# Half of the spare raw buffer for the second output weights' blocks, one sample's rows loaded behind them, and the last pages joined, in the last stage of a hybrid decoder step

## The chip, the cores and the metric

The kernel runs on one core of a Trainium2 chip. The metric is the device time of one execution in microseconds (us). The core has five engines with instruction queues of their own: PE (TensorE, matmuls and transposes; PEld is its weight load), DVE (VectorE), ACT (ScalarE), POOL (GpSimd) and SP (SyncE, which here only issues transfers). An engine works through its queue in order, and semaphores tie the queues together. DMA transfers are issued by SP and by POOL.

## The reference, cut to what matters

One step of a decoder layer for a prompt of 1,024 rows and for eight samples of one row each. All of them are projected, mixed by three head groups, and sent through one output projection:

```python
cat = concat([o_nsa * silu(z_nsa), o_rw * silu(z_rw), o_mem * silu(z_mem)])   # width 1024
return cat @ w_out                                                            # (1024, 1024), plus the residual
```

The change lies where two pieces of this meet, the prompt's output projection and the NSA group of the eight samples. For one sample (`nsa_decode_seq`), `pool[pt_row]` gathers eight pages of 128 past rows by the page table; each row holds k and v for compression and k and v for selection:

```python
cmp2 = compress(rows)                     # 32-row blocks, stride 16, through a small MLP -> compressed k, v
p    = softmax(q . ck)                    # over the compressed blocks
imp  = p @ ov                             # importance of the 16 blocks of 64 rows
sel  = top-16 blocks (first, last two forced)
o    = g0 * (p @ cv) + g1 * (softmax(q . k_sel) @ v_sel) + g2 * window
```

Everything is in float32. The large matmuls are done in three parts: each operand is split into a high part and a low part, and high x high, high x low and low x high are summed.

## The kernel before, in words

The kernel has three stages. The change touches only the last (`phase3`), which runs from about 817 us of the profiled execution to its end.

Two pieces of work share the engines there. **The fill** is the prompt's output projection (`out_prompt`): 16 tiles, eight row blocks for the second half of the output columns (weights W1) and then eight for the first half (weights W0). A tile is 24 matmuls called `p_out` (eight blocks k of the contraction, three parts each). Around it stand a split of the next `cat` block on ACT (`chi`) and DVE (`clo`), a load of the residual (`xres`) and a store, both issued by POOL. **The main line** is the samples' NSA group (`sample_nsa`). It takes the samples in two rounds, 0 to 3 (a=0) and 4 to 7 (a=1). Per sample `squeeze` runs the compression's first layer as 32 matmuls `p_hid`, 16 in the program's text; per round `p_ss` gives the scores of the selected rows, and `nsa_four` goes on with `p_co`, `p_ckT`, `p_cs`, `p_cT`, `p_imp` (twice), `p_PT`, `p_os`, `p_oT`, each a short piece of PE with a DVE and ACT piece behind it. The DVE piece behind the second `p_imp` is the longest: the scores `s_sel`, their maximum `rs_m`, ACT's exponential, and the scaling of `s_sel`, which `p_PT` needs.

The order on PE is written out by hand. The main line is a generator that yields numbers of microseconds; after each yield as many groups of three `p_out` are placed as fill that many by a clock of the program's own. So the yields (`WAIT` after each `squeeze`, and the constants in `nsa_four`) say how much fill covers the work of the other engines. The instructions of the other queues are ordered by a scheduler at build time, main line first.

Three things about memory matter.

- **Weights.** `wo_half` loads a block k of W1 or W0 as 128 x 512 raw numbers, then splits it: ACT makes `woh`, DVE makes `wol`. W1's eight raw blocks go to `raw`, a buffer of two halves (`raw[:, 0]` and `raw[:, 1]`, called `wraw` in the profile). W0's raw blocks go, by POOL's queue, to `wor`, a pool of three buffers. The split parts of W0 take the place of W1's, block by block: block k of W0 can be split when the last tile with W1 has used block k. Four blocks of W1 are loaded a second time for the samples' own projection (`again`, `wob`, raw parts in `big[:, 0]`), and four more by the `wor` pool.
- **Pages.** A sample's pages go to two tiles of 128 x 2048, X (for the compression) and KV (for the selection), each made up of eight pages. `big` has five such tiles (`pg` in the profile), to which come two from the attention stage's buffers and the two halves of `raw`. `load(s)` brings X and KV of a page in one DMA of 256 KB (line 1856); `load_x` and `load_kv` bring one of them, 128 KB each (line 1860).
- **SP's order.** SP issues pages and weights in program order, each page behind a read of the page table.

Of the kernel before, what the change touches and what calls it, by code (L numbers as in the profile page):

```python
# [10 lines left out]
F32 = mybir.dt.float32  # L11
# [25 lines left out]
RATE = {i: (0.8, 0.8, 1, 1) if i > 3 else (1.5, 1.5, 1.5, 0) for i in range(8)}  # L37
WAIT = (15.0, 5.0, 5.0, 0.0, 0.0, 0.0, 9.0, 2.0)
WARM = 34
# [75 lines left out]
class Step:  # L115
# [1759 lines left out]
    def sample_nsa(self):  # L1875
# [3 lines left out]
        with ExitStack() as ctx:  # L1879
# [4 lines left out]
            self.W1 = self.wo_half(self.wo_tiles(self.wop), 1, nc.sync, range(8),  # L1884
                                   lambda k: raw[:, k // 4, k % 4 * 512:k % 4 * 512 + 512])
            vn = dp.tile([128, 2, 128], F32, name="v_new")
            new = O["nsa_rows_sample"]
# [5 lines left out]
            for a in range(2):  # L1893
                for k in range(4):
                    s = 4 * a + k
# [3 lines left out]
            with P("snsx") as xp:  # L1899
                big = xp.tile([128, 5, 2048], F32, name="pg")  # L1900

                at = {1: (0, 2), 2: (1, 3), 3: (0, 4)}
                kvs = lambda x: x.rearrange("p (n c) -> p n c", n=8)
# [21 lines left out]
                for a in range(2):  # L1925
                    hid = dp.tile([128, 4, 2, 64], F32, name="shid")
                    if a == 0:
                        for s in range(4):
                            if s:
                                load(s)  # L1930
                            squeeze(s, hid)
                            yield WAIT[s]
                        for s in (4, 5):
                            self.pages(s, big[:, 5 - s], raw[:, s - 4])
                            X[s], KV[s] = big[:, 5 - s], kvs(raw[:, s - 4])
                        load_x(7, self.arena(0, "pg")[:])
                    else:
                        squeeze(4, hid)
                        load_x(6, big[:, 1])
                        load_kv(6, big[:, 2])  # L1940
                        load_kv(7, big[:, 3])
                        for s in (5, 7, 6):
                            squeeze(s, hid)
                            yield WAIT[s]
                        again = [self.k1p.tile([128, 2048], F32R, name="wob", tag=f"k{j}") for j in (0, 2)]
                        parts = iter([x[:, k * 512:k * 512 + 512] for x in again for k in range(4)])
                        W1 = self.wo_half(lambda name: next(parts), 1, nc.sync, range(4, 8),
                                          lambda k: big[:, 0, k * 512:k * 512 + 512])
                    VS = [KV[s] for s in range(4 * a, 4 * a + 4)]
                    pS = [self.pS.tile([128, 512], F32, name="p_ss", tag="s") for _ in range(2)]  # L1950
                    for h in range(2):
                        for k in range(4):
                            PE.matmul(pS[h][32 * k:32 * k + 32], self.qb[:, 4 * a + k, :], VS[k][:, 4 * h:4 * h + 4, 0:128],
                                      start=True, stop=True)
                    yield from self.nsa_four(a, hid, pS, VS, vn, dp)
                    if a == 0:
                        self.sample_cats()
                        yield None
# [4 lines left out]
    def nsa_four(self, a, hid, pS, VS, vn, dp):  # L1963
# [13 lines left out]
        o = self.norm_rope(ck[:].rearrange("p s d -> p (s d)")[:, None, :], 3, 1, 4, 9)  # L1977
        yield 7.0
        pk = self.pT.tile([128, 4, 128], F32, name="p_ckT", tag="t")
# [3 lines left out]
        V.tensor_copy(kt[:], pk[:64])  # L1983
        yield 1.3
        pc = self.pM.tile([128, 128], F32, name="p_cs", tag="m")
# [31 lines left out]
        V.tensor_scalar(sc[:], sc[:], self.gr[:, a, 0:1], None, op0=OP.mult)  # L2017
        yield 7.5
        srcs = [sl[:, j * 128:(j + 1) * 128] for j in range(8)] + [sc[:]]
# [12 lines left out]
        V.scalar_tensor_tensor(oS[:], vn[:, a, :], sl[:, 1024:1025], po[:], op0=OP.mult, op1=OP.add)  # L2032
        yield 1.3
        pt = self.pM.tile([128, 4, 32], F32, name="p_oT", tag="m")
# [163 lines left out]
    def wo_half(self, tiles, n, queue, ks=range(8), raws=None):  # L2198
        nc = self.nc
        out = {}  # L2200
        for k in ks:
            wl, wh = tiles(f"wol{k}"), tiles(f"woh{k}")
            raw = self.wst.tile([128, 512], F32, name="wor")[:] if raws is None else raws(k - ks[0])
            self.last_wor = queue.dma_start(raw, self.I["w_out"][0, k * 128:(k + 1) * 128, n * 512:(n + 1) * 512])
            nc.scalar.activation(wh, raw, AF.Copy, scale=0.5)  # L2205
            nc.vector.scalar_tensor_tensor(wl, raw, 0.5, wh.bitcast(F32), op0=OP.mult, op1=OP.subtract)  # L2206
            out[k] = wh, wl
        return out
# [67 lines left out]
    def out_prompt(self):  # L2276

        yield from self.out_proj_prompt(1, self.W1)
        self.W0 = self.wo_half(self.wo_tiles(self.wop), 0, self.nc.gpsimd)
        self.half = 1  # L2280
        yield from self.out_proj_prompt(0, self.W0)
# [117 lines left out]
```

## Time and profile before

| | |
|---|---|
| median of 3 runs | 976.06 us (974.77 to 979.17) |
| the profiled execution: its own time | 983.03 us |
| its span, from the first to the last instruction | 981.3 us |
| mean TensorE clock granted | 0.984 |
| PE busy | 939.0 us (96%) |
| DVE busy | 656.6 us (67%) |
| ACT busy | 443.1 us (45%) |
| DMA moved | 103.82 MB, mean 106 GB/s |

Times are in us of the profiled execution, counted from the start of its span. In the timeline a row is: start, duration, engine, line, operation, what it writes and reads, count, and in brackets the idle time of the engine before it with what ended that. In the chain of waits a row is start, duration, what. In the windows a row is a stretch, its length, then busy time of the engines (with the number of instructions), the clock granted to PE (1.00 is full), the mean busy share of the 16 DMA engines, and GB/s. Matmul ends are modelled and overlap the next one's start, so the distance from start to start is what one costs.

### The profile page before, as it was taken

The page shows a single profiled execution, that of the slowest core. Times are in us where ns is not written, and L with a number is a line of the kernel's source. Part 1 is how long each engine was busy: PE and PEld are TensorE (multiplying, and loading weights), DVE is VectorE, ACT ScalarE, POOL GpSimd, SP SyncE. Part 2 cuts the span into 40 slices and gives each one's busy share as a digit, 9 for nine tenths or more (in the row PEclk, how much of TensorE's full clock was granted, in tenths as well). Part 3 has the DMA queues.
Part 4 walks back from the last instruction along what each step waited for, and adds up shares of the span by engine and source line. Part 5 has one row for each costly group of instructions (what it writes and reads, how often), then busy time and mean ns, then how long its engine had stood idle before and what let it go on. Part 6 is the DMA issues. An engine that isn't in the chain of part 4 may idle for free.

```text
span 981.3 us, 24739 instructions
## 1 busy us (share of the span) xinstructions
PE 939.0 (96%) x9851; PEld 796.3 (81%) x9851; DVE 656.6 (67%) x2025; ACT 443.1 (45%) x990; POOL 178.9 (18%) x270
## 2 busy tenths in 40 slices
PE   7999999989999998999998999999999999998997
PEld 7998888868898887778887888888888887876775
DVE  6768669846593897644438776765768986356454
ACT  5755224232432342223435766667567675223311
POOL 2000000000000000000103444445446663112010
PEclk8999999999999999999997999999999999999999
DMA  8331303311331126146238325141110139875611
GB/s 288 87 87 33 92 21 114 97 52 55 86 99 36 40 81 156 45 120 184 61 94 234 108 66 178 62 121 40 52 38 16 43 90 272 272 235 173 202 67 36
DMA packets 134092, 103.82 MB, mean 106 GB/s; under 512 B 34833, under 2 KB 121368, under 8 KB 133848
## 3 DMA queue, kind: packets, MB, share of 16 engines
q1 hardware_dynamic: 129016, 90.53, 31.4%
q0 software_dynamic: 3200, 10.49, 3.0%
q8 instruction: 78, 1.28, 0.5%
q10 hardware_dynamic: 1760, 1.21, 0.4%
q14 instruction: 38, 0.31, 0.1%
HBM read 83.61 MB, written 22.78 MB: 108 GB/s over the span
## 4 chain that ended last, share of the span: by engine, by line
PE 72%; DVE 15%; ACT 6%; DMA 3%; issue 2%; SPq 1%; POOL 0%; DVEq 0%; ACTq 0%; POOLq 0%
PE p_pr L87 20%; PE p_pr L284 7%; PE p_out L87 6%; PE p_s L87 6%; PE p_pT L87 4%; PE p_o L87 4%; PE p_hid L87 3%; ACT p L1324 2%; DVE p L1323 2%; PE p_iy L87 2%; PE p_sc L87 2%; PE p_z L87 1%; PE p_it L87 1%; PE p_mo L1077 1%; PE p_w L203 1%
## 5 line engine op out<-in xcount | busy, mean ns | idle before, releaser
L87 PE MATMUL p_pr<-h,whi 128*128 128x512 f32 (+5 forms) x928 | 231.0, 340 | 0.1
L87 PEld LDWEIGHTS p_pr<-h,whi 128*128 128x128 f32 (+1 forms) x928 | 147.4, 184 | 18.8 <-issue 2.7
L87 PE MATMUL p_pr<-h,wlo 128*128 128x512 f32 (+5 forms) x464 | 152.5, 329 | 0.0
L1349 POOL TENSOR_SCALAR p<-p,fac,gates 128x640 f32<-128x640 f32 (+7 forms) x128 | 103.7, 821 | 108.5 <-DVE fac L1346 62.1
L1324 ACT ACTIVATE p<-p,nm 128x640 f32<-128x640 f32 (+7 forms) x128 | 93.0, 728 | 54.9 <-DVE nm L1323 48.4
L87 PEld LDWEIGHTS p_pr<-h,wlo 128*128 128x128 f32 (+1 forms) x464 | 85.1, 183 | 9.6
L284 PE MATMUL p_pr<-h,whi 128*128 128x256 f32 (+2 forms) x416 | 88.7, 309 | 0.1
L87 PE MATMUL p_pT<-ident,p 128*128 128x128 f32 x528 | 71.7, 281 | 4.6 <-ACT pt L1294 1.6
L998 POOL MEMSET w2d<- 128x128 f32 x1 | 0.2, 205 | 400.9 <-PE p_yy L87 400.9
L1323 DVE CUSTOM_DVE_ANT_0 p<-p_s,bmask 128x512 f32<-128x512 f32 (+7 forms) x96 | 60.4, 662 | 19.2 <-PE p_s L87 17.1
L284 PEld LDWEIGHTS p_pr<-h,whi 128*128 128x128 f32 x416 | 67.8, 193 | 3.3 <-ACT whi L273 0.4
L87 PEld LDWEIGHTS p_pT<-ident,p 128*128 128x128 f32 x528 | 57.9, 142 | 15.4 <-issue 6.8
L87 PE MATMUL p_o<-pt,vs 128*64 128x128 f32 x1056 | 68.1, 277 | 0.4 <-DVE cat L1382 0.4
L87 PE MATMUL p_s<-kh,qs 128*128 128x512 f32 (+3 forms) x191 | 67.7, 366 | 0.0
L274 DVE TENSOR_TENSOR wlo<-wraw,whi 128x1024 fp32r<-128x1024 f32 (+1 forms) x34 | 40.7, 1197 | 36.7 <-ACT whi L273 36.7
L284 PE MATMUL p_pr<-h,wlo 128*128 128x256 f32 (+2 forms) x208 | 63.6, 307 | 0.1
L87 PEld LDWEIGHTS p_o<-pt,vs 128*64 128x64 f32 x1056 | 57.1, 137 | 7.2 <-issue 3.8
L87 PE MATMUL p_s<-kl,qs 128*128 128x512 f32 (+3 forms) x192 | 62.4, 345 | 0.0
L273 ACT ACTIVATE whi<-wraw 128x1024 fp32r<-128x1024 f32 (+1 forms) x35 | 36.3, 1038 | 50.4 <-PE p_pr L87 36.7
L1296 DVE COPY pt<-p_pT 128x512 f32<-128x512 f32 (+1 forms) x72 | 48.3, 674 | 13.8 <-PE p_pT L87 13.0
L87 PE MATMUL p_out<-woh,chi 128*128 128x512 f32 x128 | 52.8, 412 | 0.5 <-ACT woh L2205 0.5
L87 PE MATMUL p_out<-wol,chi 128*128 128x512 f32 x128 | 50.7, 396 | 0.5 <-DVE wol L2206 0.5
(544 smaller groups left out, 1963.5 us busy)
## 6 DMA issues: line engine op xcount, KB each, us to landing
wraw<-in_w_in_dram SPq DMA_DIRECT2D x34, 512.0 KB, 3.8
pg<-in_c_pool_dram SPq DMA_DIRECT2D x64, 128.0 KB, 2.4
pg<-in_c_pool_dram SPq DMA_DIRECT2D x24, 256.0 KB, 3.6
x<-in_x_prompt_dram SPq DMA_DIRECT2D x8, 512.0 KB, 7.5
z_d<-zt SPq DMA_DIRECT2D x16, 256.0 KB, 3.1
cat<-z_d SPq DMA_DIRECT2D x8, 512.0 KB, 5.7
xres<-in_x_prompt_dram POOLq DMA_DIRECT2D x16, 256.0 KB, 3.9
out_dram<-xres POOLq DMA_DIRECT2D x16, 256.0 KB, 3.2
```

The source lines that it names most:

```text
L87: self.last = getattr(self.engine, op)(*a, **k)
L203: self.nc.tensor.matmul(ps[:, :128], self.ident[:], self.ident[:], start=True, stop=True)
L273: nc.scalar.activation(hi[:, :, :n], raw[:, :, :n], AF.Copy)
L274: (low or nc.vector).tensor_tensor(lo[:, :, :n], raw[:, :, :n], hi[:, :, :n].bitcast(F32), op=OP.subtract)
L284: self.last_mm = self.pe.matmul(ps[:m, :b - a], w[:, k, :m], h[k][:, a:b], start=(k == 0 and i == 0), stop=(k == 7 and i == 2))
L998: nc.gpsimd.memset(w2d[:], 0.0)
L1077: PE.matmul(po[t][:], a, w[:, j], start=(k + j == 0 and i == 0), stop=(k + j == 7 and i == 2))
L1296: nc.vector.tensor_copy(pt[:, :n], ps[:, :n])
L1323: V.tensor_tensor_reduce(halves(x), halves(ps), m, -1.0, 3.0e38, op0=OP.add, op1=OP.min, accum_out=nm[:, h, b:b + 1])
L1324: A.activation(x, x, AF.Exp, scale=-1.0, bias=nm[:, h, b:b + 1], accum_out=sm[:, h, b:b + 1])
L1349: nc.gpsimd.tensor_scalar(x, x, f[:, h, b:b + 1], gate[:, hd + h, 1 + b:2 + b], op0=OP.mult, op1=OP.mult)
```

## The change

Six edits, all in the last stage. Line numbers grow by one from about line 1886 and by two from about 1950.

1. The raw parts of W0's blocks 0 to 3 go to `raw[:, 1]`; blocks 4 to 7 stay with the three `wor` buffers.
2. `raw[:, 1]` is therefore not free for sample 5's KV in the first round. Its X is still loaded there; its KV is loaded in the second round, behind the splits of W0's blocks 0 to 3.
3. Sample 7's KV comes ahead of sample 4's `squeeze`.
4. Sample 6's X and KV come by eight joined DMAs (`load(6)`) in place of sixteen.
5. The four repeated W1 loads are issued behind the last page.
6. The yields change. After the `squeeze` of sample 6 stands 0.5 in place of 9.0, after that of 7 2.5 in place of 2.0; in `nsa_four` 7.0, 1.3, 7.5 and 1.3 become 8.0, 1.9, 9.5 and 2.1.

```diff
-WAIT = (15.0, 5.0, 5.0, 0.0, 0.0, 0.0, 9.0, 2.0)
+WAIT = (15.0, 5.0, 5.0, 0.0, 0.0, 0.0, 0.5, 2.5)
...
+            self.raw0 = [raw[:, 1, k * 512:k * 512 + 512] for k in range(4)] + [None] * 4
...
-                at = {1: (0, 2), 2: (1, 3), 3: (0, 4)}
+                at = {1: (0, 2), 2: (1, 3), 3: (0, 4), 6: (1, 2)}
...
-                        for s in (4, 5):
-                            self.pages(s, big[:, 5 - s], raw[:, s - 4])
-                            X[s], KV[s] = big[:, 5 - s], kvs(raw[:, s - 4])
+                        self.pages(4, big[:, 1], raw[:, 0])
+                        X[4], KV[4] = big[:, 1], kvs(raw[:, 0])
+                        load_x(5, big[:, 0])
                         load_x(7, self.arena(0, "pg")[:])
                     else:
+                        load_kv(5, raw[:, 1])
+                        load_kv(7, big[:, 3])
                         squeeze(4, hid)
-                        load_x(6, big[:, 1])
-                        load_kv(6, big[:, 2])
-                        load_kv(7, big[:, 3])
+                        load(6)
                         for s in (5, 7, 6):
                             squeeze(s, hid)
                             yield WAIT[s]
...
-                        W1 = self.wo_half(lambda name: next(parts), 1, nc.sync, range(4, 8),
-                                          lambda k: big[:, 0, k * 512:k * 512 + 512])
+                        with tc.issue_after(self.last_page.ins):
+                            W1 = self.wo_half(lambda name: next(parts), 1, nc.sync, range(4, 8),
+                                              lambda k: big[:, 0, k * 512:k * 512 + 512])
...
-        yield 7.0
+        yield 8.0
...
-        yield 1.3
+        yield 1.9
...
-        yield 7.5
+        yield 9.5
...
-        yield 1.3
+        yield 2.1
...
-            raw = self.wst.tile([128, 512], F32, name="wor")[:] if raws is None else raws(k - ks[0])
+            raw = self.wst.tile([128, 512], F32, name="wor")[:] if raws is None or raws(k - ks[0]) is None else raws(k - ks[0])
...
-        self.W0 = self.wo_half(self.wo_tiles(self.wop), 0, self.nc.gpsimd)
+        self.W0 = self.wo_half(self.wo_tiles(self.wop), 0, self.nc.gpsimd, raws=lambda k: self.raw0[k])
```

How the queues read at two places, before and now.

**POOL and DVE around W0.** POOL, before, at the start of the stage (`wor` is a raw block of W0, `xres` a residual):

```order
L2204 DMA wor<-in_w_out_dram 128x512 x3
L2223 DMA xres<-in_x_prompt_dram 128x512 x3
L2225 DMA out_dram<-xres 128x512
L2223 DMA xres<-in_x_prompt_dram 128x512
```

and now:

```order
L2206 DMA wor<-in_w_out_dram 128x512 x3
L2225 DMA xres<-in_x_prompt_dram 128x512 x3
L2206 DMA wraw<-in_w_out_dram 128x512 x4
L2227 DMA out_dram<-xres 128x512
L2225 DMA xres<-in_x_prompt_dram 128x512
```

Seven of W0's eight raw blocks are now issued at the start of the stage, where it was three; one (block 7) stays behind, at the tile in which W1 ends. DVE in the first round, before, from the scores to their scaling (`wol_12313` is block 3 of W0, `wol_12319` block 4, `wol_12325` block 5):

```order
L2014 TENSOR_TENSOR s_sel<-p_ss,im 128x512 x2
L2224 TENSOR_TENSOR xres<-xres,p_out 128x512
L1704 TENSOR_REDUCE rs_m<-s_sel 128x1
L2206 SCALAR_TENSOR_TENSOR wol_12313<-wor,woh_12314 128x512
L2206 SCALAR_TENSOR_TENSOR wol_12319<-wor,woh_12320 128x512
L2206 SCALAR_TENSOR_TENSOR wol_12325<-wor,woh_12326 128x512
L1707 RECIPROCAL rs_s<-rs_s 128x1
L2232 TENSOR_TENSOR clo<-cat_7441,chi 128x1024
L1709 TENSOR_TENSOR rs_s<-rs_s,gr 128x1
L1710 TENSOR_SCALAR s_sel<-s_sel,rs_s 128x1025
```

and now (`wol_12319` is block 6, `wol_12325` block 7):

```order
L2208 SCALAR_TENSOR_TENSOR wol_12319<-wor,woh_12320 128x512
L2016 TENSOR_TENSOR s_sel<-p_ss,im 128x512 x2
L2208 SCALAR_TENSOR_TENSOR wol_12325<-wor,woh_12326 128x512
L1704 TENSOR_REDUCE rs_m<-s_sel 128x1
L2234 TENSOR_TENSOR clo<-cat_7441,chi 128x1024
L2226 TENSOR_TENSOR xres<-xres,p_out 128x512
L2234 TENSOR_TENSOR clo<-cat_8136,chi 128x1024
L1707 RECIPROCAL rs_s<-rs_s 128x1
L1709 TENSOR_TENSOR rs_s<-rs_s,gr 128x1
L1710 TENSOR_SCALAR s_sel<-s_sel,rs_s 128x1025
```

All of W0's splits now stand ahead of `rs_m`, and two `clo` and an `xres` between `rs_m` and the scaling.

**PE and SP around sample 6.** On PE the `squeeze` of sample 6 is the last of the round. Before, 39 `p_out` followed it; the last of them and what comes behind:

```order
L87 MATMUL p_out<-woh_12308,clo 128x512
L87 MATMUL p_ss<-wraw,qb 32x512 x2
L87 MATMUL p_ss<-pg,qb 32x512 x2
L87 MATMUL p_ss<-wraw,qb 32x512 x2
L87 MATMUL p_ss<-pg,qb 32x512 x2
L87 MATMUL p_co<-w2d,shid 128x128 x4
```

and now, from that `squeeze` on:

```order
L87 MATMUL p_hid<-pg,w1a 128x128 x16
L87 MATMUL p_out<-woh_12320,chi 128x512
L87 MATMUL p_out<-wol_12319,chi 128x512
L87 MATMUL p_out<-woh_12320,clo 128x512
L87 MATMUL p_ss<-wraw,qb 32x512 x2
L87 MATMUL p_ss<-pg,qb 32x512 x2
L87 MATMUL p_ss<-wraw,qb 32x512 x2
L87 MATMUL p_ss<-pg,qb 32x512 x2
L87 MATMUL p_co<-w2d,shid 128x128 x4
```

Three `p_out` are left there; the other 36 stand in other gaps. SP before, among the KV loads (each behind a read of the page table):

```order
L1860 DMA pg<-in_c_pool_dram 128x256
L2204 DMA pg<-in_w_out_dram 128x512
L1852 TENSOR_LOAD pt
L1860 ISA
L1860 DMA pg<-in_c_pool_dram 128x256
```

and now, at the end of the pages:

```order
L1852 TENSOR_LOAD pt
L1856 ISA
L1856 DMA pg<-in_c_pool_dram 128x2x256
L2206 DMA pg<-in_w_out_dram 128x512 x4
L2263 DMA xres<-in_x_sample_dram 8x512 x2
```

The four weight loads no longer stand between the pages. Over the whole fill the number of `p_out` is the same, 384; between the program's steps they now stand as follows (`p_hid` counted in the program's text, groups of 16):

| after | `p_out` before | `p_out` now |
|---|---|---|
| `p_co`, round 0 / round 1 | 30 / 30 | 36 / 36 |
| `p_ckT` | 6 / 6 | 9 / 9 |
| `p_cs` | 15 / 15 | 15 / 15 |
| `p_cT`, first `p_imp` | 6, 6 / 6, 6 | 6, 6 / 6, 6 |
| second `p_imp` | 33 / 33 | 42 / 42 |
| `p_PT` | 9 / 9 | 9 / 9 |
| `p_os` | 6 / 6 | 9 / 0 |
| `p_hid` of samples 4, 5 and 7 | 9 | 12 |
| `p_hid` of sample 6 | 39 | 3 |

## The prediction

> **What bounds the kernel now.** I read the page first (engines, chain of waits), then stretches of 20 us over the last stage, and where PE is not full there, the timelines of the engines.
>
> ```profile
> PE 72%; DVE 15%; ACT 6%; DMA 3%; issue 2%; SPq 1%; POOL 0%; DVEq 0%; ACTq 0%; POOLq 0%
> 880.00:900.00 20.00, 16.80 (x70) 12.05 (x69) 14.95 (x29) 9.74 (x14) 4.83 (x9) 0.91 0.64 216
> 900.00:920.00 20.00, 20.00 (x218) 19.12 (x217) 8.62 (x31) 5.17 (x16) 1.59 (x3) 1.00 0.37 114
> 920.00:940.00 20.00, 17.43 (x78) 11.92 (x78) 9.49 (x24) 5.63 (x9) 2.16 (x4) 0.91 0.55 176
> ```
>
> PE carries the chain of waits. In the last stage its matmuls are the same before and after, so the change can only win what PE loses to waits and to a lower clock: 3.2 us idle in 880 to 900, 2.6 in 920 to 940, each with a clock of 0.91 (behind it in a row stand DMA share and GB/s). The places, and the price of one tile and one sample without a wait:
>
> ```profile
> 845.03 5.49 PE p_out L87 x24
> 841.46 3.57 PE p_hid L87 x32
> 865.85 0.47 PE L87 MATMUL p_out<-woh,chi 128*128 128x512 f32 x1
> 873.61 0.63 PE L87 MATMUL p_ckT<-ident,nr_o 128*64 128x128 f32 x4 [0.67 <-DVE nr_o L376]
> 875.94 0.42 PE L87 MATMUL p_cs<-ckt,q 64*32 64x128 f32 x8 [0.31 <-DVE ckt L1983]
> 883.07 0.48 PE L87 MATMUL p_out<-woh,chi 128*128 128x512 f32 x1
> 890.51 0.50 PE L87 MATMUL p_out<-woh,chi 128*128 128x512 f32 x1 [0.50 <-ACT woh L2205]
> 894.78 1.09 PE L87 MATMUL p_PT<-ident,s_sel 128*128 128x128 f32 x8 [1.86 <-DVE s_sel L1710]
> 896.34 0.77 PE L87 MATMUL p_out<-woh,chi 128*128 128x512 f32 x1
> 899.99 1.96 PE L87 MATMUL p_os<-pg,PTs 128*32 128x128 f32 x64
> 863.08 1.92 PE L87 MATMUL p_ss<-pg,qb 128*32 128x512 f32 x16
> 929.04 0.62 PE L87 MATMUL p_ss<-wraw,qb 128*32 128x512 f32 x2
> 933.53 1.89 PE L87 MATMUL p_ss<-pg,qb 128*32 128x512 f32 x2 [2.57 <-DMA pg<-in_c_pool_dram]
> 937.00 0.48 PE L87 MATMUL p_out<-woh,chi 128*128 128x512 f32 x1
> 961.58 1.09 PE L87 MATMUL p_PT<-ident,s_sel 128*128 128x128 f32 x8 [0.65 <-DVE s_sel L1710]
> ```
>
> A `p_out` costs 5.49 / 24 = 0.229 us. **First loss:** the 33 `p_out` from 883.07 should take 7.56 and `p_PT` starts 11.71 later: 4.15 lost, to W0's splits and then to `s_sel`. **Second:** the nine `p_out` from 896.34 to 899.99 take 3.65 where 2.06 is due: 1.6 lost. **Third:** `p_ss` and `p_co` of the second round take 937.00 - 929.04 = 7.96, against 865.85 - 863.08 = 2.77 in the first: 5.2 lost, to KV pages of samples 6 and 7 that come late. Small ones: 0.67 and 0.31 in the first round, 0.65 in the second.
>
> **The second loss is the clock.** Stretches of 2 us, PE alone (length, busy, clock, DMA share, GB/s):
>
> ```profile
> 897.00:899.00 2.00, 2.00 (x6) 0.50 0.54 176
> 960.00:962.00 2.00, 1.35 (x9) 1.00 0.35 131
> ```
>
> It halves after the wait of 1.86 and, by the mean of 0.91 over 920 to 940, after that of 2.57; it stays full after the one of 0.65. The Trainium skill (TensorE: Matmul & The Clock Gate, "Why this matters for your kernels") warns only of idle gaps over about 3 us; by that a new wait under 2 us would be free of it, where the row after the 1.86 wait shows a halved clock, so here the row decides.
>
> **W0's blocks (edit 1).** Why are W0's splits late now? ACT waits for raw blocks:
>
> ```profile
> 883.89 1.90 POOL L2204 DMA_DIRECT2D wor<-in_w_out_dram  x3 [1.51 <-DVE im L2005]
> 891.48 0.54 POOL L2204 DMA_DIRECT2D wor<-in_w_out_dram  x1 [1.43 <-DVE wol L2206]
> 894.47 0.63 ACT L2205 ACTIVATE woh<-wor 128x512 fp32r<-128x512 f32 x1 [1.13 <-DMA wor<-in_w_out_dram]
> wor<-in_w_out_dram POOLq DMA_DIRECT2D x8, 256.0 KB, 5.4
> 888.54 0.68 DVE L2206 SCALAR_TENSOR_TENSOR wol<-wor,woh 128x512 fp32r<-128x512 f32 x1
> 887.41 1.22 DVE L1704 TENSOR_REDUCE rs_m<-s_sel 128x1 f32<-128x1025 f32 x1
> 892.65 1.21 DVE L2232 TENSOR_TENSOR clo<-cat,chi 128x1024 fp32r<-128x1024 f32 x1
> 893.96 0.76 DVE L1710 TENSOR_SCALAR s_sel<-s_sel,rs_s 128x1025 f32<-128x1025 f32 x1
> ```
>
> Five of eight loads are issued only as `wor` buffers come free, from 883.89 to 891.48, and land 3.0 (891.48 to 894.47) to 5.4 later. The change leaves one of these, block 7, behind block 4's split. I put the new order on the old clock. From 865.85 PE runs 36 + 9 + 15 + 6 + 6 `p_out` (16.5) and some 1.2 of small matmuls, so the 42 `p_out` start at 883.6. Both small waits of this round (0.67, 0.31) lie under the six and three extra `p_out`: **1.0 gained**. DVE's splits, 0.6 apart as before, reach block 4 at about 885.4; block 7 is issued then, lands at 888.4 to 890.8, say 889.6, and is split at 890.9 (ACT 0.63, DVE 0.68). Only then follow on DVE `rs_m` (892.0), `clo` (893.2), `xres` (893.8), the second `clo` (894.9) and the scaling (896.0). PE wants the first of those `clo` with its 33rd `p_out`, at 883.6 + 32 x 0.229 = 890.9, and waits to 893.2; `p_PT` starts at 896.0, where 883.6 + 9.6 = 893.2 was due. So 2.8 stays lost of 4.15: **1.35 gained**; with the block at 888.4 it is 2.9, at 890.8 it is 0.1. The wait is cut into pieces with matmuls between them, so I take the full clock behind it, as after the 0.65 wait: **1.6 gained**, or nothing.
>
> **The same loads, earlier.** The four early blocks, 1 MB, now go out at about 828 to 831, once W1's splits have emptied the half buffer, into the busiest stretch of the DMA engines (the first two rows are of 822 to 845):
>
> ```profile
> DMA packets 5636, 7.20 MB, mean 313 GB/s; under 512 B 495, under 2 KB 4785, under 8 KB 5635
> pg<-in_c_pool_dram SPq DMA_DIRECT2D x16, 256.0 KB, 5.9
> 829.52 3.67 SPq L1856 DMA_DIRECT2D pg<-in_c_pool_dram  x4
> 845.06 0.54 SPq L1856 DMA_DIRECT2D pg<-in_c_pool_dram  x1
> 853.36 0.54 SPq L1856 DMA_DIRECT2D pg<-in_c_pool_dram  x1
> DMA to landing us min/median/max: 3.5/3.6/8.4
> ```
>
> 1 MB at 313 GB/s is 3.4 us of delay for the pages of samples 1 and 2. Sample 1's are due at 841.46. Its last one is one of the four issued from 829.52 on, 1.04 apart: at 831 or so, and with 5.9 to landing there at 837. Sample 3's last, issued at 853.36, lands at 857.0, and its `squeeze`, two tiles and two samples behind sample 1's (2 x (5.49 + 3.57) = 18.1), starts at 859.6. Margins 4.5 and 2.6, and the 3.4 fall on the first. I take nothing; without the cover it is up to 2. The Trainium skill (DMA: Bandwidth & Descriptors, "Issuing engines are not separate DMA queues") speaks against this edit: loads from POOL interleave with SP's on the same 16 engines. By it the 3.4 fall on the pages in full, which the margin of 4.5 still holds.
>
> **Sample 6 (edits 2 to 5 and the 0.5).** Only three `p_out` are left ahead of `p_ss`, so KV must come with X. Sample 5's KV goes out at about 882 to 889, behind W0's early splits, sample 7's as `p_os` frees its tile (901.6 at the latest by the times below), eight in 6.7; PE needs neither before 922. The joined loads of sample 6 wait for sample 4's `p_hid`, whose X they overwrite:
>
> ```profile
> 903.69 10.88 PE L87 MATMUL p_hid<-pg,w1a 128*128 128x128 f32 x96
> 907.46 12.32 SPq L1860 DMA_DIRECT2D pg<-in_c_pool_dram  x15
> 919.88 0.38 SPq L2204 DMA_DIRECT2D pg<-in_w_out_dram  x1
> 922.79 0.64 ACT L2205 ACTIVATE wob<-pg 128x512 fp32r<-128x512 f32 x1 [0.31 <-DMA pg<-in_c_pool_dram]
> ```
>
> Before, SP starts at 907.46, when the first 32 of 96 are done. Now: 896.0 + 1.56 (`p_PT`) + 2.06 + 2.1 (`p_os`) + 2.06 + 0.1 + 3.57 gives 907.45, the same moment. Call it t. PE reaches sample 6 at t + 7.1 + 12 x 0.229 = t + 9.9. The eighth joined load goes out at t + 8.3 (845.06 to 853.36; 7.3 at 1.04 each, as above) and lands 3.5 or 3.6 later: t + 10.8 to t + 11.9. So a **new wait of 0.9 to 2.0** stands ahead of the last `squeeze`; I take 1.5. Behind it the repeated W1 blocks (issue to ACT 2.9) queue on ACT ahead of sample 6's own pieces; `p_co` could wait up to 0.9 for them, I take **0.3**. `p_ss` itself waits no more: **5.2 gained**. POOL and SP have nothing urgent behind.
>
> **The other yields.** Nine more `p_out` (2.06) behind the second `p_imp` cover the 0.65 of the second round: **0.65 gained**. With none behind the last `p_os`, `p_oT` waits some 0.5 for DVE, and a wait of about that for the last tile's bank goes (below): nothing.
>
> ```profile
> 971.58 2.05 PE L87 MATMUL p_out<-wob,c_s 128*40 128x512 f32 x8 [0.49 <-DVE xres L2224]
> ```
>
> **Sum:** 1.0 + 1.35 + 1.6 + 5.2 - 1.5 - 0.3 + 0.65 = 8.0 us. The profiled execution took 983.03 (span 981.3), 7 above the median of the runs; the change would make it 975.0. The waits are the same in the shorter runs, so the median goes from 976.06 to **968.1**. With the best end of each term 10.4 (965.7), with the worst and 2 at the early pages 3.6 (972.5).
>
> **Rivals.**
> A. *The clock halves all the same,* behind the split of W0 (speaks for it: 2.8 of waits next to transposes; against: they come in pieces). That takes the 1.6 back: 6.4, 969.7. If it also falls at sample 6: 4.8, 971.3.
> B. *The wait only moves,* from `p_ss` to sample 6's `p_hid`, because the joined loads land as the slowest row of their kind, 8.4: t + 16.7, a wait of 6.8 in place of 1.5, and a halved clock (1.6): 1.1 is left, 975.0. For it: the pages, 1 MB of weights and the residuals come together there; against: 114 to 176 GB/s ran in 900 to 940 before, and 8.4 stands among loads that shared the 313 above.
> C. *Slower: full DMA engines.* If landing grows to 8.4 wherever loads have been put together: sample 3's pages land at 861.8, 2.2 late, plus 1.6 of clock; block 7 lands 3.7 later and keeps the clock low (5.3); sample 6 as in B (6.9): 16.0 against 8.0, **984.1**. Beyond the clock terms each us of landing costs about two (block 7 and sample 6), so it turns slower from a landing of about 6 on.
> D. *The early blocks do nothing,* since block 7 lands late and DVE's order puts `rs_m` behind it: 1.35 and 1.6 go, 5.05, 971.0.
>
> **Chances.** Forecast 0.58; A 0.18, D 0.07; B 0.10; C 0.07. Likeliest 968.1, its own range 965 to 971; for 8 in 10 I reach up into A, D and B: 964.5 to 974.5. A difference of 0.5% (4.9 us), about what a measurement of this kernel tells from no change, lies at 971.2. Faster: the forecast, most of A and half of D, 0.77; same: the rest of these and B, 0.16; slower: C, 0.07.
>
> **What would show it.** In the profile after: no `p_ss` wait for `pg` and about 2.8 us from its start to the `p_out` behind `p_co` (else B or C); `p_hid` of sample 6 waiting 0.9 to 2.0 for DMA; the clock at 1.00 around `p_PT` of both rounds (else A); W0's blocks 0 to 6 split without a wait for DMA, `p_PT` of the first round at about 896 (later than 897: D); `squeeze` of samples 1 to 3 still at 841.5, 850.5 and 859.6 (else C). The forecast is wrong if joined loads take over 1.2 us each to issue, or if DVE, not DMA, holds PE between 883 and 896 for more than 4 us.

## The result, and the profile after

The changed kernel took 972.0 us (median of ten runs, 968.98 to 974.77), the kernel before, run beside it, 977.96 (ten runs, 974.28 to 984.8): a ratio of 0.9932 with a 95% interval of 0.9909 to 0.9954, so **6.6 us faster** by the ratio (the two medians lie 6.0 apart). Run once more beside the experiments below it took 973.41 against 979.09, ratio 0.9957 (0.9927 to 0.9987), 4.2 us by the ratio. The forecast was 8.0 us and 968.1. Of the two gains, 4.2 and 6.6, neither is the better one: the intervals overlap.

The profiled execution has a span of 970.9 us (before 981.3) and a mean clock of 0.995 (before 0.984). Windows of 20 us over the part that mattered (length, then busy time of PE, PEld, DVE, ACT and POOL with the number of instructions, clock, DMA share, GB/s):

```profile
880.00:900.00 20.00, 17.64 (x141) 13.29 (x140) 12.77 (x26) 6.56 (x10) 3.53 (x7) 1.00 0.54 180
900.00:920.00 20.00, 18.36 (x141) 17.07 (x141) 8.84 (x30) 6.63 (x17) 1.30 (x3) 1.00 0.72 229
```

PE still idles some 2 us in each, at full clock now. In 920 to 940, where it idled 2.6, it is busy for 19.70. The same places as in the prediction, PE's timeline of the changed kernel:

```profile
881.19 0.48 PE L87 MATMUL p_out<-woh,chi 128*128 128x512 f32 x1
888.10 0.50 PE L87 MATMUL p_out<-woh,chi 128*128 128x512 f32 x1 [0.51 <-ACT woh L2207]
891.09 0.50 PE L87 MATMUL p_out<-woh,clo 128*128 128x512 f32 x1 [1.08 <-DVE clo L2234]
893.88 1.09 PE L87 MATMUL p_PT<-ident,s_sel 128*128 128x128 f32 x8 [0.19 <-DVE s_sel L1710]
895.41 0.48 PE L87 MATMUL p_out<-woh,chi 128*128 128x512 f32 x1
897.67 1.96 PE L87 MATMUL p_os<-pg,PTs 128*32 128x128 f32 x64
917.38 3.81 PE L87 MATMUL p_hid<-pg,w1a 128*128 128x128 f32 x32 [1.64 <-DMA pg<-in_w_out_dram]
921.82 0.62 PE L87 MATMUL p_ss<-wraw,qb 128*32 128x512 f32 x2
924.68 0.71 PE L87 MATMUL p_co<-w2d,shid 128*128 128x128 f32 x4 [0.30 <-DVE shid L1020]
925.15 0.48 PE L87 MATMUL p_out<-woh,chi 128*128 128x512 f32 x1
952.87 1.03 PE L87 MATMUL p_PT<-ident,s_sel 128*128 128x128 f32 x8
```

Read from start to start at 0.229 us a `p_out`. The 42 `p_out` from 881.19 should take 9.6 and take 12.69: 3.1 are lost (before 4.15 of 33). The nine behind `p_PT` take 2.26 (before 3.65). `p_ss` and `p_co` take 925.15 - 921.82 = 3.33 (before 7.96, without a wait 2.77). Ahead of sample 6's `p_hid` stands a new wait: twelve `p_out` from 912.73 on take 4.65, 1.9 more than due. `p_PT` of the second round waits for nothing. From the first round's `p_ss` (860.37, before 863.08) to the end of the span it is 110.5 us, before 118.2: **7.7 gained in this stage**, in these two executions. The other 2.7 us between the two spans fall ahead of the place that changed.

Why 3.1 us are left in the first round, from the timelines of POOL, ACT and DVE:

```profile
883.12 0.54 POOL L2206 DMA_DIRECT2D wor<-in_w_out_dram  x1 [1.61 <-DVE im L2010]
887.42 0.63 ACT L2207 ACTIVATE woh<-wor 128x512 fp32r<-128x512 f32 x1 [3.66 <-DMA wor<-in_w_out_dram]
888.69 1.21 DVE L1704 TENSOR_REDUCE rs_m<-s_sel 128x1 f32<-128x1025 f32 x1
893.07 0.75 DVE L1710 TENSOR_SCALAR s_sel<-s_sel,rs_s 128x1025 f32<-128x1025 f32 x1
```

Block 7, the one raw block that stayed behind, is issued at 883.12 and is there for ACT at 887.42. `rs_m` stands behind its split on DVE, and the scaling that `p_PT` needs behind that.

And why sample 6 is late, from SP's timeline (sample 7's KV, sample 6, the repeated W1 loads):

```profile
898.14 6.97 SPq L1860 DMA_DIRECT2D pg<-in_c_pool_dram  x8
905.86 7.87 SPq L1856 DMA_DIRECT2D pg<-in_c_pool_dram  x8
913.83 1.98 SPq L2206 DMA_DIRECT2D pg<-in_w_out_dram  x4
```

SP issues with hardly a break from just behind the start of `p_os` (897.67) to 915.8. The row of `p_hid` names a weight load as the end of its wait. It was the last of the eight pages, issued at 913.18: ACT, idle, takes up the first of those weights only at 918.91, 1.5 us behind the start of `p_hid`, and the run with sample 6 first confirms it.

```profile
918.91 1.27 ACT L2207 ACTIVATE wob<-pg 128x512 fp32r<-128x512 f32 x2 [4.88 <-DMA pg<-in_w_out_dram]
```

### The profile page after: what moved, and what is told of

The parts are those of the page before. It is cut to its first block, busy times and chain, and to the rows that moved or that the text cites. A ratio compares the mean times of both kernels' runs of the same rounds, so it can differ in the third digit from the quotient of the medians.

```text
span 970.9 us, 24716 instructions
## 1 busy us (share of the span) xinstructions
PE 929.7 (96%) x9851; PEld 789.3 (81%) x9851; DVE 655.6 (68%) x2025; ACT 442.1 (46%) x990; POOL 179.3 (18%) x270
## 4 chain that ended last, share of the span: by engine, by line
PE 65%; DVE 15%; issue 6%; ACT 5%; DMA 5%; SPq 1%; POOL 1%; DVEq 0%; POOLq 0%; ACTq 0%
PE p_pr L87 19%; PE p_pr L284 8%; PE p_s L87 5%; PE p_pT L87 4%; PE p_o L87 4%; PE p_out L87 4%; ACT p L1324 2%; DVE p L1323 2%; PE p_iy L87 2%; PE p_z L87 1%; DMA out_dram<-xres 1%; PE p_it L87 1%; PE p_w L203 1%; PE p_mo L1077 1%; DVE pt L1296 1%
## 5 line engine op out<-in xcount | busy, mean ns | idle before, releaser
L87 PE MATMUL p_out<-woh,clo 128*128 128x512 f32 x128 | 50.2, 392 | 1.1 <-DVE clo L2234 1.1
```

The lines of the kernel that those rows point to most:

```text
L87: self.last = getattr(self.engine, op)(*a, **k)
```

## The experiments

Ratios are against the kernel before, run on the same chip in the same comparison. The changed kernel itself was run beside the kernel before twice, the second time in one comparison with "block 7 early", "sample 6 first" and "both"; the other runs are set against it by their ratios, each of which is good to some 0.003 (3 us). Two groups: parts of the change alone, and single causes.

### Parts of the change

**Edits 1 and 2 alone.**

```diff
+            self.raw0 = [raw[:, 1, k * 512:k * 512 + 512] for k in range(4)] + [None] * 4
...
+                        load_kv(5, raw[:, 1])
                         squeeze(4, hid)
...
```

> The kernel before with edits 1 and 2 alone (W0's blocks 0 to 3 in the half buffer, sample 5's KV behind their splits); pages of sample 6 and all yields as before. My theory: block 7 still comes late behind block 4's split, and only 33 p_out stand behind the second p_imp, so p_PT of the first round waits for s_sel in one piece, about 2.9 us (893.5 against 890.6 on the old clock), and the half clock behind it (1.6) stays. The 5.2 us at p_ss of the second round stay too. Gain 1.3 us, ratio 0.9987. Rival (the early blocks alone remove the whole second loss of 4.15 us and the half clock): gain 5.7 us, ratio 0.994.

Measured: 981.73 against 980.78, ratio 1.0021 (0.9993 to 1.0048): no gain. PE's timeline:

```profile
892.19 1.97 PE L87 MATMUL p_PT<-ident,s_sel 128*128 128x128 f32 x8 [3.87 <-DVE s_sel L1710]
930.42 1.02 PE L87 MATMUL p_ss<-pg,qb 128*32 128x512 f32 x2 [2.50 <-DMA pg<-in_c_pool_dram]
```

No `p_out` waits for W0 any more; the whole wait has moved behind them, to `p_PT`, where it is longer than the 2.9 expected (the 33 `p_out` from 880.57 take 11.62, 4.07 lost, against 4.15 before). With 33 `p_out` behind the second `p_imp` the DVE chain of `s_sel` is what ends last, and it is no shorter. The half clock, from 891.83 to 895.24, comes behind that wait: `p_PT` takes 1.97 in place of 1.09, and the nine `p_out` behind it 2.72 in place of 2.06. The wait of 2.5 at `p_ss` stays, here at full clock: `p_ss` and `p_co` take 6.28 us, 3.5 more than without a wait, where the kernel before lost 5.2 with the same wait and a half clock behind it. The rival of a gain of 5.7 falls.

**Edits 3, 4 and 5 alone.**

```diff
...
+                        load_kv(7, big[:, 3])
                         squeeze(4, hid)
-                        load_x(6, big[:, 1])
-                        load_kv(6, big[:, 2])
-                        load_kv(7, big[:, 3])
+                        load(6)
...
+                        with tc.issue_after(self.last_page.ins):
...
```

> The kernel before with edits 3, 4 and 5 alone (sample 7's KV early, sample 6 joined, W1 loads behind the last page); W0 and all yields as before, so 9 p_out ahead of sample 6's p_hid and 39 behind it. My theory: p_ss of the second round no longer waits (5.2 us gained), but p_hid of sample 6 comes at t + 9.2 and its pages at t + 11.8, so it waits about 2.6 us in one piece and the clock halves there (1.6): net gain 1.0 us, ratio 0.999; 2.6 us (0.9973) if the clock stays full. Rival (the joined loads remove the third loss for good): gain 5.2 us, ratio 0.9947, no wait over 1 us at p_hid.

Measured: 981.82, ratio 1.0021 (0.9994 to 1.0049). From PE's and SP's timelines (the first row is of the first round):

```profile
893.02 1.09 PE L87 MATMUL p_PT<-ident,s_sel 128*128 128x128 f32 x8 [1.85 <-DVE s_sel L1710]
916.60 6.57 PE L87 MATMUL p_hid<-pg,w1a 128*128 128x128 f32 x32 [3.09 <-DMA pg<-in_w_out_dram]
922.92 0.47 PE L87 MATMUL p_out<-woh,chi 128*128 128x512 f32 x1
904.88 7.88 SPq L1856 DMA_DIRECT2D pg<-in_c_pool_dram  x8
```

`p_ss` waits no more, but `p_hid` of sample 6 waits 3.1, and its 32 matmuls take 6.3 in place of 3.57, under a half clock from 915.56 to 922.39. The third loss has moved by one step and kept its size. With more fill ahead of sample 6 the wait would be shorter, and the yields of before put 9 `p_out` there and 39 behind.

The first round is a second sample of the kernel before: up to `p_os` the engines have the same instructions in the same order. The 33 `p_out` from 882.22 take 10.80 us to `p_PT`, so 3.25 are lost where the profile before shows 4.15, and the clock stays full behind them.

**Edit 6 alone.** All yields of the change, loads as before.

> The kernel before with edit 6 alone (all yields of the change), loads as before. My theory: 36 p_out (8.2 us) that stood ahead of p_ss in the second round and hid its pages are gone from there, so the wait at p_ss grows from 5.2 to about 13.4 us; the waits of 0.98 and 0.65 us are covered and the one of 4.15 falls a little (to 3). Slower by about 5.4 us, ratio 1.0055. Rival (the yields carry the gain by themselves, the loads are accessory): faster by 3 to 6 us, ratio 0.994 to 0.997.

Measured: 985.74, ratio 1.0053 (1.0019 to 1.0086), slower as expected. The page wait at `p_ss` has grown:

```profile
929.80 1.03 PE L87 MATMUL p_ss<-pg,qb 128*32 128x512 f32 x1 [4.47 <-DMA pg<-in_c_pool_dram]
```

`p_ss` and `p_co` take 13.39 us there (924.27 to 937.66), 10.6 more than without a wait (expected 13.4; some of it is at sample 6's `p_hid` now, 1.03 idle).

**All loads, no yields.** The changed kernel with `WAIT` and `nsa_four`'s yields of before.

> The changed kernel with all yields put back (edits 1 to 5 without 6). My theory: the loads alone leave the small waits (0.98 and 0.65 us), a wait of 2.9 us in one piece at the first p_PT and one of 2.6 us at sample 6's p_hid, each with a half clock (1.6): gain 2.4 us, ratio 0.9975; with the clock full behind both 5.6 us, ratio 0.9943. Rival (the yields only trim the small waits): within 1.7 us of the changed kernel, gain 5 us or more, ratio 0.995 or less, with no wait over 2 us.

Measured: 982.19, ratio 1.0001 (0.9972 to 1.0031): nothing is left of the gain. PE's timeline:

```profile
891.72 1.97 PE L87 MATMUL p_PT<-ident,s_sel 128*128 128x128 f32 x8 [3.30 <-DVE s_sel L1710]
918.39 5.34 PE L87 MATMUL p_hid<-pg,w1a 128*128 128x128 f32 x32 [3.91 <-DMA pg<-in_w_out_dram]
```

The waits of the two load parts stand side by side, each as one piece, each with a half clock (890.89 to 897.72 and 918.2 to 921.61). So neither loads nor yields show a gain alone: 1.0001 and 1.0053, together 0.993 to 0.996.

**The yields behind the squeezes alone put back**, on the changed kernel:

```diff
-WAIT = (15.0, 5.0, 5.0, 0.0, 0.0, 0.0, 0.5, 2.5)
+WAIT = (15.0, 5.0, 5.0, 0.0, 0.0, 0.0, 9.0, 2.0)
```

> The changed kernel with the yields behind the squeezes alone put back (9.0 and 2.0), nsa_four's yields as changed. My theory: the fill is a fixed budget, 384 p_out. With 39 of them spent ahead of p_ss again, only 18 of 42 are left behind the second p_imp of the second round, and p_PT waits 5.5 us there; sample 6's p_hid waits 2.6 in place of 1.9, and half clocks come behind both. About 8 us slower than the changed kernel, ratio to before about 1.001. Rival (the 39 p_out only cover work elsewhere, what counts is the sum of waits for pages): within 1 us of the changed kernel, ratio 0.993 to 0.996.

Measured: 978.96 against 980.67, ratio 0.9975 (0.9948 to 1.0001), by the ratios some 2 to 4 us slower than the changed kernel, not 8.

```profile
954.12 0.48 PE L87 MATMUL p_out<-woh,chi 128*128 128x512 f32 x1
960.59 1.72 PE L87 MATMUL p_PT<-ident,s_sel 128*128 128x128 f32 x8 [2.11 <-DVE s_sel L1710]
```

The 18 `p_out` are there, and the wait behind them, but of 2.4 us and not 5.5: with no `cat` split left to do on DVE, its chain from `p_imp` to `s_sel` takes 6.5 us, where I had set 9.6, what the 42 `p_out` take. Sample 6's `p_hid` loses 2.7, as expected (2.6). The budget is fixed, as expected; the price was too high.

### Single causes

**The changed kernel once more,** for comparison on one chip.

> The changed kernel once more, beside the three that follow, so that they can be set against it on one chip. Ratio to the kernel before 0.993, as at first, if the 6.6 us are the kernel's own; another chip or another pattern of half clocks would show as more than 0.003 from that.

Measured: 973.41, ratio 0.9957 (0.9927 to 0.9987), within 0.003 of the first, so the gain is the kernel's own; whether it is 4 or 7 us this does not tell. PE's waits are the same to 0.2 us (1.06 for `clo`, 1.46 ahead of sample 6).

**Block 7 early.** W0's blocks 0 to 2 in `wor`, 3 to 6 in the half buffer, so that block 7 follows block 0.

```diff
-            self.raw0 = [raw[:, 1, k * 512:k * 512 + 512] for k in range(4)] + [None] * 4
+            self.raw0 = [None] * 3 + [raw[:, 1, k * 512:k * 512 + 512] for k in range(4)] + [None]
```

> The changed kernel with W0's blocks 0 to 2 in the three wor buffers and blocks 3 to 6 in the half buffer, so that block 7's load waits for block 0's split (about 880) and not for block 4's (883.1). My theory: what is left of the second loss, 3.1 us in the 42 p_out of the first round, is block 7 landing at 887.3; issued at 880 it lands at about 884.2, rs_m starts at 886.2 in place of 888.7, and 2.4 us of the 3.1 go. Ratio to the changed kernel 0.9975, to before 0.9907. Rival (the loss is DVE's order, s_sel's scaling behind two clo and an xres, whenever block 7 lands): under 0.5 us gained, ratio to before 0.993.

Measured: 971.58, ratio 0.9922 (0.9894 to 0.9949), beside 0.9957 for the changed kernel; the intervals overlap, so the trace has to tell. From POOL's, DVE's and PE's timelines:

```profile
879.12 0.54 POOL L2206 DMA_DIRECT2D wor<-in_w_out_dram  x1 [1.91 <-DVE im L2003]
885.61 1.22 DVE L1704 TENSOR_REDUCE rs_m<-s_sel 128x1 f32<-128x1025 f32 x1
890.81 1.09 PE L87 MATMUL p_PT<-ident,s_sel 128*128 128x128 f32 x8 [0.23 <-DVE s_sel L1710]
```

The load goes out at 879.12, `rs_m` starts 5.5 us behind the first of the 42 `p_out` (880.10) in place of 7.5, and they take 10.71: 1.1 is lost in place of 3.1 (2.0 gained, 2.4 expected). So the block is the cause of 2.0 of the 3.1. The 1.1 that stay are DVE's order, as the rival had it for the whole: DVE has no gap over 0.2 us there.

**Sample 6 first.**

```diff
-                at = {1: (0, 2), 2: (1, 3), 3: (0, 4), 6: (1, 2)}
+                at = {1: (0, 2), 2: (1, 3), 3: (0, 4), 6: (2, 4)}
...
+                        load(6)
                         load_kv(7, big[:, 3])
                         squeeze(4, hid)
-                        load(6)
```

> The changed kernel with sample 6's X and KV in tiles 2 and 4 of the five, which come free with p_os of the first round, and its joined loads ahead of sample 7's KV. My theory: the wait ahead of sample 6's p_hid (1.9 us) is the row of issues on SP, 16 pages from p_os on with sample 6 last; put first, its pages are issued from about 899 to 907 and land by 911, 6 us ahead of need, and sample 7's KV lands by 918, 4 us ahead of p_ss. Gain 1.9 us, ratio to the changed kernel 0.998, to before 0.9912. Rival 1 (the pages are late by landing, with weights and pages on the same DMA engines): the wait stays over 1 us, ratio 0.993. Rival 2 (the wait moves to p_ss, for sample 7's KV): p_hid free, p_ss waits 1 us or more, ratio 0.993.

Measured: 971.48, ratio 0.9933 (0.9903 to 0.9962). SP's timeline, and PE's at sample 6 (the first 12 matmuls of its 32):

```profile
900.31 9.00 SPq L1856 DMA_DIRECT2D pg<-in_c_pool_dram  x8
909.82 6.23 SPq L1860 DMA_DIRECT2D pg<-in_c_pool_dram  x8
917.69 1.50 PE L87 MATMUL p_hid<-pg,w1a 128*128 128x128 f32 x12
```

The wait is gone and has not moved to `p_ss`, so the pages and the row of issues on SP held `p_hid`, not the weights, which are issued later here (from 916.15) than in the changed kernel (913.83). The profiled execution is no shorter (971.0), because a half clock fell on the first round in it, of which the last section tells.

**Both,** block 7 early and sample 6 first.

> Both edits of the two runs before together. My theory: the two places do not touch each other, so 2.4 and 1.9 us add up to 4.3: ratio to the changed kernel 0.9956, to before 0.9888, with PE losing under 1 us at each of the two places. Rival (as with the parts of the change itself, one gain pays for the other, or half clocks take the place of the waits): no better than the better of the two alone, ratio to before 0.991 or more.

Measured: 969.53 (967.38 to 971.04), ratio 0.9907 (0.9874 to 0.994): beside the changed kernel 0.005 less, where 0.0044 was expected. At the two places PE loses 1.1 us, all of it in the 42 `p_out` (expected under 1 each); neither row has a wait worth naming:

```profile
890.58 1.09 PE L87 MATMUL p_PT<-ident,s_sel 128*128 128x128 f32 x8 [0.21 <-DVE s_sel L1710]
912.22 3.73 PE L87 MATMUL p_hid<-pg,w1a 128*128 128x128 f32 x32
```

Here the gains add up. It is the fastest of all that were run: 3.9 us under the changed kernel's 973.41 by the medians, though the two intervals overlap.

**Both, with all yields of before.**

> The kernel with block 7 early and sample 6 first (the two edits together), with all yields of the kernel before. My theory: with all loads on time what is left is DVE's and ACT's chains, and these the yields must cover: 0.98 us at p_ckT and p_cs, about 3.2 us at p_PT of the first round (10.85 us of chain against 33 p_out), 0.7 and 0.65 in the second: 3.7 us slower than with the changed yields, ratio to before 0.9945, up to 0.9963 with a half clock behind the 3.2. Rival (yields were needed only because loads came late): within 1 us of the kernel with the changed yields, ratio to before 0.99 to 0.9917.

Measured: 976.84, ratio 0.995 (0.993 to 0.9971), as expected, beside 0.9907 with the changed yields.

```profile
893.07 1.09 PE L87 MATMUL p_PT<-ident,s_sel 128*128 128x128 f32 x8 [3.03 <-DVE s_sel L1710]
```

The chain from the second `p_imp` to `p_PT` takes 10.8 us, as with the changed yields (10.7), and 33 `p_out` cover 7.6 of it where 42 cover 9.6. Even with every load on time the old yields leave 3 us at `p_PT`. What these yields cover is DVE's chain, not late loads.

**Edit 5 undone.**

```diff
-                        with tc.issue_after(self.last_page.ins):
-                            W1 = self.wo_half(lambda name: next(parts), 1, nc.sync, range(4, 8),
+                        W1 = self.wo_half(lambda name: next(parts), 1, nc.sync, range(4, 8),
```

> The changed kernel with edit 5 undone: the four repeated W1 loads go out on SP as before by the scheduler's order, here behind the third of sample 6's eight joined pages. My theory: they wait for sample 5's X to be used up (about 909.3) and hold the other five pages behind them, so the last page is issued at about 916 in place of 913.2 and lands at 920; the wait ahead of sample 6's p_hid grows from 1.9 to about 4.5 us, and a window of half clock (1.7) comes behind it: 2.6 to 4.3 us slower than the changed kernel, ratio to before 0.997 to 0.999. Rival (the loads are few and cheap, edit 5 does nothing, or frees p_co of its wait): within 0.7 us of the changed kernel, ratio 0.993 to 0.996.

Measured: 977.33, ratio 0.9966 (0.9937 to 0.9994). SP's and PE's timelines (of `p_hid` the first ten of 32):

```profile
905.57 3.06 SPq L1856 DMA_DIRECT2D pg<-in_c_pool_dram  x3
909.15 1.78 SPq L2205 DMA_DIRECT2D pg<-in_w_out_dram  x4
911.44 4.72 SPq L1856 DMA_DIRECT2D pg<-in_c_pool_dram  x5
919.58 1.68 PE L87 MATMUL p_hid<-pg,w1a 128*128 128x128 f32 x10 [4.12 <-DMA pg<-in_c_pool_dram]
```

The four weight loads wait for sample 5's X and hold five pages behind them; the last page is issued at 916 and the wait is 4.4 us by the distance of starts (expected 4.5), with a half clock behind it (920.45 to 923.86). The time alone does not decide, since the ratio lies between the two that were expected; by the trace four small DMAs at the wrong place in a queue cost 2.5 us of waiting, and edit 5 takes that away.

**Edit 4 undone.**

```diff
-                        load(6)
+                        load_x(6, big[:, 1])
+                        load_kv(6, big[:, 2])
```

> The changed kernel with edit 4 undone: sample 6's X by eight DMAs of 128 KB, then its KV by eight more. My theory: X alone is issued from 905.9 to 912.9 and lands by 915.4, so p_hid of sample 6 waits no more (1.9 us gained), but KV is issued to 920 and lands by 922.5, and p_ss, now due at 919.9, waits 2.6 us, and the W1 loads behind it come at 920 to 922 and hold p_co or what follows: 0.7 us slower than the changed kernel, up to 2.5 with a half clock; ratio to before 0.994 to 0.997. Rival (joining is what removes the third loss): p_ss waits 5 us or more, ratio to before 0.998 or more.

Measured: 977.95, ratio 0.9976 (0.9954 to 0.9998). From PE's and ACT's timelines:

```profile
929.21 1.05 PE L87 MATMUL p_ss<-pg,qb 128*32 128x512 f32 x4 [0.97 <-DMA pg<-in_c_pool_dram]
930.03 0.63 ACT L2208 ACTIVATE wob<-pg 128x512 fp32r<-128x512 f32 x1 [3.27 <-DMA pg<-in_w_out_dram]
943.19 0.65 PE L87 MATMUL p_ckT<-ident,nr_o 128*64 128x128 f32 x4 [3.65 <-DVE nr_o L376]
```

`p_hid` of sample 6 waits no more, as expected, and `p_ss` waits about 1 us where 2.6 was expected. The price is elsewhere: the repeated W1 loads, behind 24 pages on SP, land at 930, and `p_ckT` waits 3.65 us behind `nr_o`. Two things make up that wait. The splits stand ahead of the norm's `nr_sq` on ACT, which starts 3.0 us behind `s_ck` (1.4 in the changed kernel). And in this build an `xres` and a `clo` stand between the norm's steps on DVE, so that `nr_o` is 8.5 us behind `nr_sq` and not 6.1. I had named the risk ("hold `p_co` or what follows") without a price for it. So by this trace joining pays through what stands behind the pages in the queue, and through the order that the scheduler then finds, more than through the pages. The profile is of the slowest of the ten runs (983.93), so what the wait costs in the others is not shown.

## Why the prediction was right, and where it was not

The direction, the places and, but for the clock, the mechanisms were right. The time, 972.0, lies in the wide range (964.5 to 974.5), which reached up into the rivals, but not in the 965 to 971 that the forecast had as its own; the kernel before had itself gone up by 1.9. The size was over by 1.4 us in the first comparison and 3.8 in the second. Times are put on the old clock by adding 863.08 - 860.37 = 2.71.

- **Small waits of the first round, 1.0:** gone. Right.
- **W0, 1.35 gained, 2.8 left:** 1.1 gained, 3.1 left, in these two executions. Block 7 was issued at 885.8 (forecast 885.4), reached ACT at 890.1 (889.6), `p_PT` came at 896.6 (896.0). The mechanism is confirmed by the run with block 7 early. The size is not firm: with edits 3 to 5 alone the instructions of the kernel before lost 3.25 here and not 4.15. The Trainium skill (DMA: Bandwidth & Descriptors, "Issuing engines are not separate DMA queues") had spoken against the early loads. The traces agree with it: the 24 pages of samples 1 to 3 land 6.6 to 8.4 us after issue, by the medians, in the eleven profiles with early blocks, and 3.6 to 5.6 in the three without. Yet the `squeeze` of sample 1, at 838.59, has the same distance to the first `p_ss` (21.8) as before (863.08 - 841.30). The cover held, so rival C's first step fell: landing did grow beyond 6, and no `squeeze` waited for it.
- **Sample 6, a new wait of 1.5 (0.9 to 2.0):** 1.9. The joined loads started at 905.86, when the `p_hid` of sample 4 had ended, as forecast. But this was close: sample 7's KV was issued to 905.1. I had let them begin at 901.6 at the latest and take 6.7, which is up to 908.3, and had not seen that this is behind the 907.45 of sample 6. With fewer `p_out` between `p_os` and `p_hid` they come to bound sample 6, which made the waits of 3.1 and 3.9 in the runs above.
- **`p_ss`, 5.2 gained, and `p_co`, 0.3 lost:** together 4.6 gained (7.96 to 3.33), forecast 4.9. `p_co` lost 0.56.
- **Second round, 0.65:** gone. Right; `p_oT` now waits 0.47 for DVE, as forecast.
- **The clock, 1.6 gained:** this is the step that failed, and with it the sentence that the waits are the same in the shorter runs. In the two profiled executions it was gained: the nine `p_out` behind `p_PT` take 2.26 us in place of 3.65. But it is no firm gain, as follows.

**How firm the clock is.** A full clock after the change is not assured. Six profiles have the changed kernel's instructions in the first round (its own two, sample 6 first, edits 4 and 5 undone, the yields behind the squeezes put back). In two of them a half clock falls there: with sample 6 first (890.54 to 897.36, behind waits of 0.84, 0.23 and 1.06, where the changed kernel had 0.51, 0.23 and 1.08) and with edit 5 undone (889.73 to 893.14). Nor does the kernel before always lose it: of the two profiles with its first round, the one of edits 3 to 5 alone had the full clock.

What the first round gained differs accordingly. From the first `p_ss` to `p_os`, with the 18 more `p_out` (4.1 us) taken off, the six take 33.2 to 35.5 us, 33.8 in the mean; the two take 36.9 and 34.6. That is 2.0 gained by the means, where the sum had 1.0 + 1.35 + 1.6 = 3.95 and the pair of profiles shows 3.7. The 5.2 at `p_ss` had such a part too: the same wait cost 3.5 at full clock (edits 1 and 2 alone).

So the sum was built on one execution in which a half clock stood at both places. The mean clocks point the same way, though they do not tell where in the kernel a half clock fell: 0.984 in that execution, 0.992 on average in 25 other runs of the kernel before and 0.991 in the twelve of the changed kernel beside them, 0.994 in the ten of the first comparison. Of the 25 runs each 0.01 of mean clock costs 6.9 us by a straight line; at a clock of 0.995 they give 976.8, the twelve of the changed kernel, by their own line, 971.7. That is **5.1 us at equal clock**, an estimate by these lines, and 4 to 7 was measured.

Three slips in the working leave the 8.0 as it is. With block 7 at 888.4 the same steps give 2.55 gained and not 2.9. The worst end of 3.6 keeps the 1.6 that the text gives as "or nothing"; without it 2.0 are left, 974.1. And in C block 7 would land 4.2 later, not 3.7.

Of the rivals, A came in two of the six profiles, at the place that A named, though in neither of the changed kernel's own. B's shape, a wait that only moves to `p_hid`, came in the runs with parts of the change, but through the row of issues on SP and not through a landing of 8.4. C did not come. D holds for the early blocks alone (4.07 lost with edits 1 and 2, 4.15 and 3.25 without) and falls for the whole: with the changed yields the 42 `p_out` lose 4.8 without early blocks (edit 6 alone, 14.43 us from 882.58) (one profile) and 3.1 to 3.4 with them, at full clock in both cases.

What the sum could not show is that no part pays alone. It added a gain to each edit; the runs give 1.002 for edits 1 and 2, 1.002 for edits 3 to 5, 1.005 for edit 6 and 1.000 for all but edit 6. Each load edit only moves its wait to the next step, and the yields are what places fill there.

## What to carry to other kernels

A load that comes earlier gains nothing until the work that covered its wait is put where the next wait will be; change loads and covers together, and measure them so. Count a queue's issues one by one up to the first that something waits for: four small loads in front of five pages cost here 2.5 us of waiting, eight pages in front of eight others 1.9. And take a gain that rests on the clock of one profiled execution as a chance, not as a term.

## What was not expected of the hardware

The half clock comes in pieces of one length. In these profiles each spell in the last stage lasts 3.41 us or a multiple (6.83, 10.24), and inside one execution the spells lie whole multiples apart (before: 895.96 and 933.51, 11 times 3.41). So the time can be laid out in windows of 3.41 us from the start of a spell. PE alone (length, busy time, clock, DMA share, GB/s), the kernel before:

```profile
892.55:895.96 3.41, 1.46 (x10) 1.00 0.67 231
895.96:899.37 3.41, 3.16 (x8) 0.50 0.46 156
899.37:902.78 3.41, 3.41 (x78) 1.00 0.21 80
```

Sample 6 first:

```profile
887.13:890.54 3.41, 1.98 (x7) 1.00 0.83 268
890.54:893.95 3.41, 2.70 (x6) 0.50 0.75 241
893.95:897.36 3.41, 3.41 (x13) 0.50 0.18 70
```

The changed kernel once more:

```profile
913.50:916.92 3.42, 1.96 (x10) 1.00 0.87 242
916.92:920.33 3.41, 3.41 (x31) 1.00 0.70 227
```

Edits 3 to 5 alone:

```profile
891.67:895.08 3.41, 1.71 (x11) 1.00 0.80 244
895.08:898.49 3.41, 3.41 (x69) 1.00 0.41 138
```

Over the last stage of all profiles of this case, the span's end aside: a full window with PE busy for less than 1.5 us (1.46 above) is always followed by a half one (11 cases), and one above 2.1 never. Between 1.7 and 2.1 both occur: 1.98 is followed by a half window, 1.96 and 1.71 are not. What decides there is open; the modelled ends of matmuls blur the busy time, and the kind of matmul may count. A half window gives way to a full one at 3.05 or more, and not at 2.70. So **what counts is how a wait falls on the windows**: 1.86 us, all of it in one, halved the clock before; 1.85 us at the same `p_PT`, cut by a border at 891.67, did not with edits 3 to 5 alone. A wait cut in pieces, which I took as safe, is so only while no window collects some 1.4 us of them.

The Trainium skill (TensorE: Matmul & The Clock Gate, Part 1, "What's actually happening") says that the clock follows a free-running window of 3413 ns; the spells agree to the hundredth. It wants an idle window for the fall to half; here one that was busy for 1.98 of 3.41 us was enough, so its advice to avoid idle gaps of more than about 3 us ("Why this matters for your kernels") is too mild for this kernel.
